# Second block's rows transposed before their norm, first weights split during the last expert, attention weights scaled as rows

## The chip, the cores and the metric

The kernel runs on one core of a Trainium2 chip. The metric is device microseconds from launch to end, the median of timed runs. Five engines work side by side and wait for one another by semaphores: TensorE (PE, matmuls; PEld is its weight load), VectorE (DVE), ScalarE (ACT), GpSimd (POOL) and SyncE (SP, which here issues the weight transfers).

## The reference, cut to what matters

Two transformer blocks on 256 rows of 1024, all in float32. Block 1 ends with a mixture of 32 experts and a norm; block 2 starts with a second norm, a projection, differential attention and a state space model, and ends with 32 larger experts.

```
x = x + hier_moe(rmsnorm(x, ffn_norm), ...)       # 32 experts, the last stage of block 1
x = rmsnorm(x, final_norm)                        # block 1's result, block 2's input
h = rmsnorm(x, norm1_g) * (1 + sc1) + sh1
q, k, v, u = split(h @ w_in)                      # 4 x 512 columns
p = softmax(causal(q k^T / 8))                    # per head two maps, 64 wide
att = p[0] - lam * p[1]                           # 4 heads
o = rmsnorm(att @ v, subln_g) * 0.8
mix = concat(o, s5(u)) @ w_out
x = x + g1 * mix
x = x + g2 * moe(rmsnorm(x, norm2_g)..., ...)     # 32 experts, top 4
out = rmsnorm(x, final_g)
```

## The kernel before

Rows stand on the partitions as `x_sb[128, 2, 1024]`, two blocks of 128 rows. Every weight passes through one pool of 20 slots of 1 MB (`Slots`, L230 to L292): SP issues a load as soon as a plan of all uses says that a slot will be free, so transfers run ahead of the work, and the first loads of the second expert stage are issued while block 2's mixer still runs. The order of the instructions on each engine is set by a planner that simulates them, except where `keep` holds the written order or `after(...)` puts what a block issues behind given instructions on the same engine. Each engine takes its own instructions in order.

The stages that the change touches, in order of time:

The last expert of block 1 (L1590 to L1646, e = 31): 4 weight tiles for gate and up, silu on ScalarE (L1614), `hid` on VectorE, a transposition, the copy `hdT` (L1631), 2 weight tiles for the down projection into `py`, and four copies of `py` into `ysb` on ScalarE (L1644). A conditional block for overfull experts (`spill1`, L1542, not taken) stands ahead of it. `heat` (L422) issues matmuls on the identity whose result nobody reads; it keeps TensorE working.

The join (L1647 to L1671): the scatter of the last four experts into `acc[0]` and `acc[1]` (two PSUM banks each, L1650), 14 heating matmuls, the split of the first weight tile u0, and the norms. A split (`split`, L446) makes of a float32 tile a high part, cast on ScalarE (L452), and a low part by subtraction on VectorE or GpSimd (L454), each in four pieces; a product then takes three matmuls (`mm3`, L461). Both norms of the join (block 1's last and block 2's first) are folded into one factor a row, from the sums of squares of `acc` and of `acc * fnorm`; the factor is put on a diagonal (L1670).

The turned rows (`turned`, L428; L1681): 16 products of x_sb, read with a stride of 8 elements, with that diagonal, which transpose and scale in one. Then, two k at a time, scale and shift by the modulation (L1687 to L1694), high part on ScalarE, low part on VectorE and GpSimd, and the splits of u1, q20 and k20 behind that.

The projections (`pair_T2`, L1708): 2 halves of 8 k of three matmuls each, half by half; u0 and u1 first, then the state space part and the q, k and v tiles in turn.

The attention heads: `d_scores` (L1813), `d_turn` (L1835), which puts the softmax denominators on diagonals and gets `p0/s0 - lam p1/s1` transposed by 6 products with them, `d_values` (L1852) and `d_out` (L1867), which scales and transposes the result by products with a diagonal of the row norm. Then the state space output, the gated unit, the output projection, the router and the 32 experts of block 2 (L2153 to L2236).

Of the kernel before, what the change touches and what calls it, by code (L numbers as in the profile page):

```python
# [19 lines left out]
D = 1024  # L20
# [289 lines left out]
def program(ctx: ExitStack, tc, T, out, plan):  # L310
# [1183 lines left out]
    sums = kpool.tile([128, 4, 2], F32, name="sums")  # L1494
    with tc.tile_pool(name="psm", bufs=1, space=PSUM) as pp, tc.tile_pool(name="m1s", bufs=2) as m1s, \
# [5 lines left out]
        px_ = lambda: pp.tile([128, 512], F32, name="px", tag="px")  # L1501
# [23 lines left out]
        def turn1(g):  # L1525
            pm = pp.tile([128, 2, 128], F32, name="pm")
# [63 lines left out]
        for e in range(32):  # L1590
            if e == 2:
                router2(px_())
            if e == 31:
                spill1()
            if e == 28:
                for _ in s5g:
                    pass
            g, e_ = divmod(e, 4)
            xe = xes[g][:, :, 32 * e_:32 * e_ + 32]
            pa = pp.tile([128, 2, 128], F32, name="pa")  # L1600
# [13 lines left out]
            act(sl, pa[:, 0], AF.Silu)  # L1614
# [13 lines left out]
            pm2 = pp.tile([128, 128], F32, name="pm2", tag="pm")  # L1628
# [26 lines left out]
        jk, jk2 = (W.alloc("jk").rearrange("p (a d) -> p a d", a=2) for _ in range(2))  # L1655
        af = [a.rearrange("p h c -> p (h c)") for a in acc]
        keep(tt(x_sb[:, 0], af[0], fnb, op=OP.mult))
        keep(act(jk[:, 0], af[0], AF.Square, accum_out=sums[:, 0, 0:1]))
        dgs = []
        for i in range(2):  # L1660
            c = slice(i, i + 1)
            keep(stt(jk2[:, i], x_sb[:, i], 1.0, x_sb[:, i], op0=OP.mult, op1=OP.mult, accum_out=sums[:, 1, c]))
            keep(ts(sums[:, 2, c], sums[:, 0, c], EPS / D, EPS * EPS, op0=OP.mult, op1=OP.add))
            keep(stt(sums[:, 3, c], sums[:, 1, c], 1.0 / D, sums[:, 2, c], op0=OP.mult, op1=OP.add))
            e_pool = keep(nc.gpsimd.tensor_tensor(sums[:, 3, c], sums[:, 3, c], mhalf[:, :1], op=OP.pow))
            if i == 0:
                keep(tt(x_sb[:, 1], af[1], fnb, op=OP.mult))
                e_act = keep(act(jk[:, 1], af[1], AF.Square, accum_out=sums[:, 0, 1:2]))
            dgs.append(jk2[:, i, :128])
            e_dve = keep(ts(dgs[i], ident, sums[:, 3, c], None, op0=OP.mult))  # L1670
# [614 lines left out]
```

## Time and profile before

| | us |
|---|---|
| timed runs, median (range) of 3 | 1894.46 (1894.25 to 1896.6) |
| the profiled execution, its own time | 1892.38 |
| its span, first to last instruction | 1890.6 |
| mean granted TensorE clock, share of full | 0.951 |
| TensorE busy, of the span | 1661.5 (88%) |
| VectorE busy | 680.5 (36%) |
| ScalarE busy | 351.8 (19%) |
| GpSimd busy | 171.3 (9%) |
| transfers, mean | 362 GB/s, 683.77 MB |

A row of a timeline has the start, the duration of what is merged in it, the engine, the line of the kernel, the operation, what it writes and reads, the shape and how many instructions; in brackets the idle time of the engine before it and what ended that. A float32 product on TensorE is two records (two passes), a transposition one. A row of a table of windows has the window, its length, and for each engine the busy time with the count of instructions, then the granted TensorE clock as a share of full speed, the share of the 16 DMA engines and GB/s. Busy TensorE is not TensorE at its peak, since the ends of matmuls are modelled.

### The profile page before, as it was taken

The numbers are of one execution on the slowest core, as the hardware profiler recorded it, in microseconds if no ns is written. First come the engines' busy times: TensorE is split into PE (matmuls) and PEld (weight loads), VectorE is DVE, ScalarE is ACT, GpSimd is POOL, SyncE is SP. The second block draws the span as 40 slices with busy tenths as digits, with TensorE's granted clock in tenths as the row PEclk, the third lists the DMA queues.
The fourth block names the chain that finished last, engine by engine and source line by source line (L and its number), as shares of the span: only waits on it lengthen the run. The fifth ranks groups of instructions, "written<-read, shape, count | busy, mean of one in ns | idle before, by whom it ended". The sixth has DMA issues, their size and how long they took to land. (4 is left out here: it accounts for less than half of the span.)

```text
span 1890.6 us, 27408 instructions
## 1 busy us (share of the span) xinstructions
PE 1661.5 (88%) x11497; PEld 906.0 (48%) x11497; DVE 680.5 (36%) x1411; ACT 351.8 (19%) x833; POOL 171.3 (9%) x150
## 2 busy tenths in 40 slices
PE   9988998978887776899799999999989989899887
PEld 8787867645553342598634333333323333333322
DVE  3886866553220000295622232222222222222221
ACT  3654533111111111254210000000000000000000
POOL 2863320000000000131200000000000000000000
PEclk9989999989998787799799999999999999999999
DMA  9445647999999999745599999999999999999994
GB/s 385 161 179 205 265 169 317 394 401 421 420 419 421 420 421 420 300 166 187 236 387 408 421 421 421 421 422 421 421 421 421 422 421 421 421 421 421 421 422 202
DMA packets 95219, 683.77 MB, mean 362 GB/s; under 512 B 10608, under 2 KB 10992, under 8 KB 12560
## 3 DMA queue, kind: packets, MB, share of 16 engines
q1 hardware_dynamic: 94464, 679.90, 87.7%
q8 instruction: 94, 1.54, 0.3%
q10 hardware_dynamic: 624, 2.03, 0.3%
q14 instruction: 37, 0.30, 0.0%
HBM read 680.84 MB, written 1.05 MB: 361 GB/s over the span
## 5 line engine op out<-in xcount | busy, mean ns | idle before, releaser
L2162 PE MATMUL pab<-wt,xe 128*64 128x512 f32 x2048 | 471.7, 598 | 18.4 <-DMA wt<-in_m2w_dram 18.4
L2162 PEld LDWEIGHTS pab<-wt,xe 128*64 128x64 f32 x2048 | 141.0, 137 | 300.8 <-issue 289.2
L2201 PE MATMUL py<-wt,hdT 128*64 128x512 f32 x1024 | 238.2, 598 | 19.8 <-DMA wt<-in_m2w_dram 17.1
L1606 PE MATMUL pa<-wt,xe 128*32 128x256 f32 x2048 | 151.0, 427 | 32.6 <-DMA wt<-in_m1w_dram 32.6
L2201 PEld LDWEIGHTS py<-wt,hdT 128*64 128x64 f32 x1024 | 69.5, 136 | 160.8 <-issue 108.7
L2175 DVE TENSOR_SCALAR gc<-pab 128x512 f32<-128x512 f32 x32 | 22.1, 691 | 339.5 <-PE pab L2168 339.5
L1606 PEld LDWEIGHTS pa<-wt,xe 128*32 128x32 f32 x2048 | 70.5, 120 | 102.8 <-DMA wt<-in_m1w_dram 43.1
L2207 DVE TENSOR_TENSOR b1b<-py,gate 64x512 f32<-64x512 f32 x64 | 44.1, 688 | 200.5 <-PE py L2201 188.6
L2177 ACT ACTIVATE sg<-gc 128x512 f32<-128x512 f32 x32 | 20.1, 630 | 461.2 <-DVE gc L2175 461.2
L1616 DVE TENSOR_TENSOR hid<-pa,sl 128x128 f32<-128x128 f32 x32 | 9.3, 290 | 240.8 <-ACT sl L1614 240.7
L1638 PE MATMUL py<-wt,hdT 128*32 128x256 f32 x1024 | 79.4, 446 | 15.0 <-issue 7.2
L402 POOL TENSOR_SCALAR r<-q 128x1 f32<-128x1 f32 x2 | 0.4, 191 | 946.6 <-DVE q L2253 946.6
L454 DVE TENSOR_TENSOR wh<-wt,wh 128x512 fp32r<-128x512 f32 (+2 forms) x57 | 76.5, 1372 | 10.8 <-ACT wh L452 10.6
L2048 PEld LDWEIGHTS pm<-gt,x_sb 128*128 128x128 f32 x512 | 62.4, 200 | 29.4 <-issue 29.0
L2048 PE MATMUL pm<-gt,x_sb 128*128 128x128 f32 x512 | 68.5, 290 | 5.1 <-DVE gt L2037 5.1
L2089 PE MATMUL pm<-b1b,st 128*128 128x512 f32 x120 | 63.7, 633 | 10.3 <-DVE b1b L2207 10.2
L1644 ACT COPY ysb<-py 32x256 f32<-32x256 f32 x128 | 46.4, 363 | 138.7 <-PE py L1638 137.5
L1522 PE MATMUL px<-gt,x_sb 128*128 128x128 f32 x256 | 65.5, 415 | 5.6 <-DVE s5t L1481 2.4
L2090 DVE TENSOR_TENSOR acc<-acc,pm 128x512 f32<-128x512 f32 x60 | 41.2, 687 | 77.7 <-PE pm L2089 77.7
L1522 PEld LDWEIGHTS px<-gt,x_sb 128*128 128x128 f32 x256 | 62.2, 335 | 12.2 <-issue 4.2
L452 ACT CAST wh<-wt 128x512 fp32r<-128x512 f32 (+2 forms) x65 | 62.0, 1019 | 14.6 <-issue 7.0
L464 PE MATMUL ps<-hTp,wh 128*128 128x256 f32 x480 | 63.4, 294 | 0.0
(577 smaller groups left out, 2007.8 us busy)
## 6 DMA issues: line engine op xcount, KB each, us to landing
wt<-in_m2w_dram SPq DMA_DIRECT2D x384, 1024.0 KB, 19.8
wt<-in_m1w_dram SPq DMA_DIRECT2D x192, 1024.0 KB, 17.7
wt<-in_wf_dram SPq DMA_DIRECT2D x44, 1024.0 KB, 8.0
wt<-in_wada_dram SPq DMA_DIRECT2D x24, 1024.0 KB, 5.0
x_sb<-in_x_dram SPq DMA_DIRECT2D x2, 512.0 KB, 4.2
out_dram<-y SPq DMA_DIRECT2D x4, 256.0 KB, 2.0
wt<-in_b_dram SPq DMA_DIRECT2D x3, 256.0 KB, 11.9
pars<-in_pars_dram ACTq DMA_DIRECT2D x1, 705.0 KB, 8.5
```

The costliest lines, as they stand in the source:

```text
L452: hi = nc.scalar.copy(h[:, a], w[:, a])
L454: lo = e.tensor_tensor(l[:, a], w[:, a], h[:, a].bitcast(F32), op=OP.subtract)
L464: mm(o, a[x], b[y], start=first and j == 0, stop=last and j == 2, skip_group_check=True)
L1522: mm(px[:, k], xkn[:, i, 4 * h + k], gts[g][:, i], start=(k == 0 and i == 0), stop=(i == 1), skip_group_check=True)
L1606: m_ = mm(pa[32 * q:32 * q + 32], xe[:, k], w[:, :, k % 2, 128 * q:128 * q + 128], start=(k == 0), stop=(k == 7), skip_group_check=True)
L1638: mm(py[32 * d:32 * d + 32], hdT[:, 32 * q:32 * q + 32], w[:, q % 2, 256 * d:256 * d + 256], start=(q == 0), stop=(q == 3), skip_group_che ...
L1644: m_copy = nc.scalar.copy(o, i)
L2048: mm(px[:, k], x_sb[:, i, 128 * kk:128 * kk + 128], gts[g][:, i], start=(k == 0 and i == 0), stop=(i == 1), skip_group_check=True)
L2089: mm(p, st2[g][:, i], ysb[g][:, 512 * d:512 * d + 512], start=True, stop=True)
L2162: last = mm(pab[a][64 * h:64 * h + 64], xe[:, k], w[:, 1024 * a + 512 * h:1024 * a + 512 * h + 512], start=(k == 0), stop=False, skip_grou ...
L2201: mm(py[d][64 * d:64 * d + 64], hdT[:, kk % 4, 64 * (kk // 4):64 * (kk // 4) + 64], w[:, kk % 2, 512 * d:512 * d + 512], start=(kk == 0), ...
L2207: tt(ysb[g][64 * e_:64 * e_ + 64, 512 * d:512 * d + 512], py[d][r_], gate2[r_], op=OP.mult)
```

## The change

Five edits. (1) u0 is split ahead of the last expert's matmuls, behind the copies of the expert before it on ScalarE and VectorE; u1 is split inside the last expert, behind its silu and hdT; all lower parts on VectorE. Two of the last expert's four copies to ysb go to VectorE. (2) Behind the scatter stand 3 heating matmuls for 14. The products with `fnorm` and the squares go half row by half row, each engine on another bank than the other. (3) The rows of x_sb are transposed unscaled, 16 transpositions (`rows`), while the sums for the norms still run; the factor is spread to a row on all partitions by two matmuls with the identity (`rb`), copied (`rbs`) and multiplied onto the turned rows (`times`) before the modulation (`high`, `low`); GpSimd has no part in it any more. The stage is written inside the expert stage's pools. (4) `pair_T2` goes k by k, both halves at each. (5) In `d_turn` the attention rows are scaled and combined as rows on VectorE and transposed by 3 transpositions; in `d_out` the same for the output, read from PSUM, so that the copy `osb` goes.

```diff
@@ last expert
             if e == 31:
                 spill1()
+                with after(m_copy, h_copy):
+                    prep2("u0")
...
-            act(sl, pa[:, 0], AF.Silu)
+            a_silu = act(sl, pa[:, 0], AF.Silu)
...
-            nc.vector.tensor_copy(hdT, pm2)
-            py = pp.tile([128, 256], F32, name="py")
+            h_copy = nc.vector.tensor_copy(hdT, pm2)
+            if e == 31:
+                with after(a_silu, h_copy):
+                    prep2("u1")
+            py = bank("py")[:, :256]
...
-                m_copy = nc.scalar.copy(o, i)
+                if e == 31 and d % 2:
+                    h_copy = nc.vector.tensor_copy(o, i)
+                else:
+                    m_copy = nc.scalar.copy(o, i)
@@ join
-        heat(px_, 14)
-        with after(m_copy):
-            prep2("u0", [nc.vector, nc.gpsimd, nc.vector, nc.gpsimd])
...
+        heat(px_, 3)
...
+        def rows(i):
+            for k in range(8):
+                keep(tr(pts[k // 2][:, k % 2, i * 128:(i + 1) * 128], xkn[:, i, k], ident))
+
+        def both_norms(i, whole):
+            q = sums[:, i]
+            c = lambda k: q[:, k:k + 1]
+            keep(tt(c(4), c(0), c(1), op=OP.add))
+            keep(ts(c(5), c(4), EPS / D, EPS * EPS, op0=OP.mult, op1=OP.add))
+            keep(stt(c(6), c(2), 1.0 / D, c(5), op0=OP.mult, op1=OP.add))
+            keep(nc.gpsimd.tensor_tensor(c(6), c(6), mhalf[:, :1], op=OP.pow))
+
+        sq = lambda i, h: keep(act(jh[:, h], acc[i][:, h], AF.Square, accum_out=sums[:, i, h:h + 1]))
+        tf = lambda i, h: keep(tt(x2[:, i, h], acc[i][:, h], f2[:, h], op=OP.mult))
+        tf(0, 0), sq(0, 1), tf(0, 1), sq(0, 0)
+        rows(0)
+        keep(act(js[:, 0], x_sb[:, 0], AF.Square, accum_out=sums[:, 0, 2:3]))
+        tf(1, 0), sq(1, 1), tf(1, 1), sq(1, 0)
+        rows(1)
+        both_norms(0, True)
+        keep(stt(js[:, 1], x_sb[:, 1], 1.0, x_sb[:, 1], op0=OP.mult, op1=OP.mult, accum_out=sums[:, 1, 2:3]))
+        both_norms(1, False)
+        rb = pp.tile([128, 2, 512], F32, name="rb", tag="acc0")
         for i in range(2):
...
+            keep(mm(rb[:, 0, 128 * i:128 * i + 128], sums[:, i, 6:7].to_broadcast([128, 128]), ident, start=(i == 0), stop=True,
+                    skip_group_check=True))
...
+        keep(nc.scalar.copy(rbs, rb[:, 0, :256]))
...
+        def times(j):
+            keep(tt(hv[:, j % 2], pts[j], rbs[:, None, :].to_broadcast([128, 2, 256]), op=OP.mult))
+
+        def high(j):
+            for a in range(2):
+                A, B = ab(2 * j + a)
+                keep(act(hp2[0][:, 2 * j + a], hv[:, j % 2, a], AF.Identity, scale=A, bias=B))
+
+        def low(j):
+            A, B = ab(2 * j + 1)
+            f = hv[:, 2 + j % 2]
+            e_ = keep(act(f[:, 1], hv[:, j % 2, 1], AF.Identity, scale=A, bias=B))
+            A, B = ab(2 * j)
+            keep(ts(f[:, 0], hv[:, j % 2, 0], A, B, op0=OP.mult, op1=OP.add))
+            return e_, keep(tt(hp2[1][:, 2 * j:2 * j + 2], f, hp2[0][:, 2 * j:2 * j + 2].bitcast(F32), op=OP.subtract))
+
+        times(0)
+        for j in range(4):
+            high(j)
+            if j < 3:
+                times(j + 1)
+            e_act, e_dve = low(j)
@@ behind the turned rows
-        with after(e_act, e_dve, e_pool):
-            prep2("u1", [nc.vector, nc.gpsimd] * 2)
+        with after(e_act, e_dve):
             prep2("q20")
@@ pair_T2
-            for b in range(2):
-                for k in range(8):
+            for k in range(8):
+                for b in range(2):
@@ d_turn
-            for m in range(2):
-                dg = fs.tile([128, 2, 128], F32, name="dg2", bufs=4)
-                for i in range(2):
-                    ts(dg[:, i], ident, st[:, 2, m, i:i + 1], None, op0=OP.mult)
...
+            for i, (a, e) in enumerate(((0, 128), (128, 384))):
+                ts(p0[:, a:e], p0[:, a:e], st[:, 2, 0, i:i + 1], None, op0=OP.mult)
+                stt(p0[:, a:e], p1[:, a:e], st[:, 2, 1, i:i + 1], p0[:, a:e], op0=OP.mult, op1=OP.add)
             pt = ps()
...
+            for a in (0, 128, 256):
+                tr(pt[:, a:a + 128], p0[:, a:a + 128], ident)
@@ d_values and d_out
-            nc.vector.tensor_copy(osb, po)
...
             for i in range(2):
-                ts(dg[:, i], ident, r[:, i:i + 1], None, op0=OP.mult)
+                ts(osb[:, i], po[:, i], r[:, i:i + 1], None, op0=OP.mult)
             pt = ps()[:, :S]
             for i in range(2):
-                mm(pt[:, 128 * i:128 * i + 128], osb[:, i], dg[:, i], start=(i == 0), stop=True, skip_group_check=True)
+                tr(pt[:, 128 * i:128 * i + 128], osb[:, i], ident)
```

## Rows read from the trace of the kernel before

**Rows 1.** Windows of 10 us where the second expert stage begins.
```profile
940.00:950.00 10.00, 10.00 (x50) 6.70 (x50) 1.37 (x4) 4.68 (x6) 0.00 (x0) 0.78 0.20 66
950.00:960.00 10.00, 10.00 (x50) 3.84 (x48) 0.00 (x0) 0.00 (x0) 0.00 (x0) 1.00 0.98 388
```

**Rows 2.** The last of the saturated windows of 30 us.
```profile
1830.00:1860.00 30.00, 28.01 (x119) 9.13 (x120) 7.67 (x12) 1.00 (x2) 0.00 (x0) 1.00 1.01 420
```

**Rows 3.** Windows by stage of block 2's mixer.
```profile
816.50:857.00 40.50, 38.42 (x317) 36.89 (x318) 35.82 (x67) 16.56 (x47) 4.24 (x3) 0.96 0.65 227
857.00:917.00 60.00, 58.07 (x711) 50.86 (x710) 32.98 (x69) 26.38 (x63) 7.60 (x12) 1.00 0.51 196
```

**Rows 4.** SyncE's issues of u0 and u1; median to landing, the same in both windows.
```profile
760.41 0.33 SPq L259 DMA_DIRECT2D wt<-in_wf_dram  x1
762.89 0.33 SPq L259 DMA_DIRECT2D wt<-in_wf_dram  x1
wt<-in_wf_dram SPq DMA_DIRECT2D x1, 1024.0 KB, 21.3
```

**Rows 5.** Timeline of ScalarE in the last expert.
```profile
780.86 0.28 ACT L1614 ACTIVATE sl<-pa 128x128 f32<-128x128 f32 x1 [14.22 <-PE pa L1606]
785.89 1.49 ACT L1644 COPY ysb<-py 32x256 f32<-32x256 f32 x4 [4.75 <-PE py L1638]
```

**Rows 6.** Timeline of the join, up to the projections u0 and u1.
```profile
786.75 3.63 PE L1650 MATMUL acc<-ysb,st 128*128 128x512 f32 x8
787.41 2.18 ACT L452 CAST wh<-wt 128x512 fp32r<-128x512 f32 x4
...
791.61 1.02 ACT L1658 ACTIVATE jk<-acc 128x1024 f32<-128x1024 f32 x1 [2.02 <-DVE x_sb L1657]
791.61 1.22 DVE L1662 SCALAR_TENSOR_TENSOR jk<-x_sb 128x1024 f32<-128x1024 f32 x1
792.53 0.19 ACT L1658 ACTIVATION_READ_ACCUMULATOR jk<-acc 128x1 f32 x1
...
792.76 0.15 DVE L1663 TENSOR_SCALAR sums<-sums 128x1 f32<-128x1 f32 x1
...
793.18 0.55 POOL L1665 TENSOR_TENSOR sums<-sums,mhalf 128x1 f32<-128x1 f32 x1 [1.61 <-DVE sums L1664]
...
795.44 7.92 PE L439 MATMUL ps<-jk,x_sb 128*128 128x128 f32 x32 [1.94 <-ACT jk L1668]
...
805.88 10.22 PE L464 MATMUL ps<-hT2p,wh 128*128 128x256 f32 x83 [0.57 <-DVE hT2p L1693]
```

**Rows 7.** TensorE's timeline; then groups by form (busy us, mean ns of one).
```profile
820.16 11.76 PE L464 MATMUL ps<-hT2p,wh 128*128 128x256 f32 x96
854.05 1.50 PE L1846 MATMUL ps<-dg,pr 128*128 128x128 f32 x12
916.46 1.03 PE L1950 MATMUL ps<-cst,x_sb 128*128 128x128 f32 x8
...
L1972 DVE TENSOR_TENSOR gm<-ps,gb 128x512 f32<-128x512 f32 x4 | 2.8, 688 | 7.0 <-PE ps L464 7.0
L1975 ACT ACTIVATE gm<-x_sb 128x512 f32<-128x512 f32 x4 | 2.5, 632 | 11.4 <-DVE x_sb L1974 11.4
L1807 DVE TENSOR_TENSOR th<-th,vz 128x256 f32<-128x256 f32 x4 | 1.7, 416 | 0.0
L469 ACT CAST cat<-th 128x256 fp32r<-128x256 f32 x4 | 1.6, 404 | 2.3 <-DVE th L1807 2.1
L1806 DVE TENSOR_SCALAR th<-th 128x256 f32<-128x256 f32 x4 | 1.1, 288 | 2.3 <-ACT th L1805 2.3
```

**Rows 8.** Granted clock in one window of 1 us during the turned rows.
```profile
798.00:799.00 1.00, 1.00 (x6) 1.00 (x5) 0.00 (x0) 0.00 (x0) 0.00 (x0) 0.50 0.00 0
```

**Rows 9.** TensorE's timeline at the first head's turn and the third head's scores.
```profile
845.39 0.77 PE L1846 MATMUL ps<-dg,pr 128*128 128x128 f32 x2 [1.78 <-ACT wh L452]
...
855.85 0.93 PE L1818 MATMUL ps<-qkT 64*128 64x128 f32 x8 [0.30 <-ACT qkT L390]
```

More of the change, by code (lines that the diff above doesn't have):

```diff
@@ L1500, in program @@
         slots4 = C("slot32").rearrange("p (a s) -> p a s", a=4)[:, None].to_broadcast([128, 2, 4, 32])
-        px_ = lambda: pp.tile([128, 512], F32, name="px", tag="px")
+        bank = lambda n: pp.tile([128, 512], F32, name=n, tag=n)
+        px_ = lambda: bank("px")
         s5g = s5_tables(s5p, px_)
@@ L1525, in turn1 @@
         def turn1(g):
-            pm = pp.tile([128, 2, 128], F32, name="pm")
+            pm = bank("pm")[:, :256].rearrange("p (i t) -> p i t", i=2)
             for i in range(2):
@@ L1599, in program @@
             xe = xes[g][:, :, 32 * e_:32 * e_ + 32]
-            pa = pp.tile([128, 2, 128], F32, name="pa")
+            pa = bank("pa")[:, :256].rearrange("p (a f) -> p a f", a=2)
             for k in range(8):
@@ L1650, in program @@
                 keep(mm(acc[i][:, h], st1[7][:, i], ysb[7][:, 512 * h:512 * h + 512], start=False, stop=True, skip_group_check=True))
-        heat(px_, 14)
-        with after(m_copy):
-            prep2("u0", [nc.vector, nc.gpsimd, nc.vector, nc.gpsimd])
[L1655 to L1658, printed above, removed]
@@ L1671, in program @@
-        W.drop()
+        heat(px_, 3)
+        jk, jk2 = (W.alloc("jk") for _ in range(2))
+        x2 = x_sb.rearrange("p i (h c) -> p i h c", h=2)
+        f2 = fnb.rearrange("p (h c) -> p h c", h=2)
+        js = jk.rearrange("p (a c) -> p a c", a=2)
+        jh = jk2.rearrange("p (a c) -> p a c", a=4)
+        pts = [bank(n).rearrange("p (a t) -> p a t", a=2) for n in ("pa", "pm", "py", "px")]
+        def rows(i):
+            for k in range(8):
+                keep(tr(pts[k // 2][:, k % 2, i * 128:(i + 1) * 128], xkn[:, i, k], ident))
@@ L1672, in program @@
+        W.drop(2)
     m1x.close()
@@ L1678, in ps @@
             return pp.tile([128, 512], F32, name="ps", tag="ps")
-        hp2 = both(halves("hT2p"), k8)
-        pts = turned(fs, ps, x_sb, None, dgs)
-        for k in range(0, 8, 2):
-            A, B = ([ab1[:, j, k + a:k + a + 1] for a in range(2)] for j in range(2))
-            hf = [jk2[:, k // 2 % 2, 256 * a:256 * a + 256] for a in (1, 2)]
-            for a in range(2):
-                keep(act(hp2[0][:, k + a], pts[k + a], AF.Identity, scale=A[a], bias=B[a]))
-            if k // 2 % 2 == 0:
-                keep(ts(hf[1], pts[k + 1], A[1], B[1], op0=OP.mult, op1=OP.add))
-            else:
-                e_act = keep(act(hf[1], pts[k + 1], AF.Identity, scale=A[1], bias=B[1]))
-            keep(ts(hf[0], pts[k], A[0], B[0], op0=OP.mult, op1=OP.add))
-            e_dve = keep(tt(hp2[1][:, k], hf[0], hp2[0][:, k].bitcast(F32), op=OP.subtract))
-            e_pool = keep(nc.gpsimd.tensor_tensor(hp2[1][:, k + 1], hf[1], hp2[0][:, k + 1].bitcast(F32), op=OP.subtract))
-        W.drop()
-        with after(e_act, e_dve, e_pool):
-            prep2("u1", [nc.vector, nc.gpsimd] * 2)
+        with after(e_act, e_dve):
             prep2("q20")
             prep2("k20", nc.gpsimd)
-            r = rstd(fs, sums[:, 0], D, 2, "r0")
+            r = rstd(fs, sums[:, :, 4], D, 2, "r0")
             for i in range(2):
@@ L1835, in d_turn @@
         def d_turn(h):
[L1836 to L1842 removed]
+            (p0, p1), st = hst[h]
+            for i, (a, e) in enumerate(((0, 128), (128, 384))):
+                ts(p0[:, a:e], p0[:, a:e], st[:, 2, 0, i:i + 1], None, op0=OP.mult)
+                stt(p0[:, a:e], p1[:, a:e], st[:, 2, 1, i:i + 1], p0[:, a:e], op0=OP.mult, op1=OP.add)
             pt = ps()
[L1844 to L1847 removed]
+            for a in (0, 128, 256):
+                tr(pt[:, a:a + 128], p0[:, a:a + 128], ident)
             ptb = fs.tile([128, 384], F32, name="ptb2")
```

33 lines of the change are left out of this document (9 added, 24 removed).

## Prediction

> **What bounds the kernel now.** I read the granted clock and the span first, then the ten-microsecond windows around the join of second mixer and second expert stage. [Rows 1] show transfers at 0.20 of the sixteen DMA engines in 940 to 950 and at 0.98 in the next window; [rows 2] is one of the thirty such windows between there and 1860, all at 1.00 to 1.02. So from about 950 the expert weights set the pace. The mixer does not: before 950 the weight slots are full and the queue waits for the first expert to empty one. Whatever brings that first expert forward brings the whole saturated stretch forward by as much. The window tables by stage then say what the mixer itself waits for: in 816.5 to 857 TensorE is busy 38.42 of 40.5 us and VectorE 35.82; in 857 to 917 TensorE 58.07 of 60 and VectorE 32.98 [rows 3]. TensorE work removed there counts nearly whole, VectorE work added before 857 does too. Between the last expert of block 1 and 806 neither holds: it is a chain of waits, read from the timeline.
>
> **The change, part by part.** Times are places in the profiled execution (1892.38 us, span 1890.6 plus 1.8 around it). The three timed runs have a median of 1894.46, so the sum is subtracted from that.
>
> *Last expert.* The first two weight tiles, u0 and u1, are issued at 760.41 and 762.89 and each lands 21.3 us later [rows 4]: 781.7 and 784.2. silu of the last expert runs at 780.86, the four copies to ysb from 785.89, 1.49 in all [rows 5]. In the forecast u0's four casts (2.18 us for four, [rows 6]) stand behind silu on ScalarE, run 781.7 to 783.9, and meet only idle time; their lower parts on VectorE (0.69 each) likewise. u1's casts run 784.2 to 786.4 and hold up the copies to ysb, of which ScalarE now has two (0.75) and VectorE two, behind u1's last lower part: ready at about 787.7 instead of 787.38, so the accumulating matmuls (3.63, [rows 6]) end near 790.9, 0.5 later than now. If the cover is missing (casts ahead of silu) it is rival B.
>
> *Norm and transposition.* Now: the diagonals wait for the row norms, 16 matmuls in two passes (32 records) take 7.92 us from 795.44, and the projections u0 and u1 end at 805.88 + 10.22 = 816.10 [rows 6]. The new chain: acc[0] is complete half-way through the accumulation, 789.1. One half product on VectorE must wait for the other engine's square on the same bank, as ScalarE's square waits 2.02 us for VectorE now [rows 6]; a square costs 0.63 [rows 7] and 0.19 for its sum [rows 6], a product 0.69 [rows 7], so row block 0 stands at 789.1 + 0.82 + 0.69 = 790.6 and its 8 transposes follow at the old strided pitch (7.92/32 = 0.25): 791.4 to 793.4. ScalarE goes on with the second square of block 0 (790.7), the square of the whole row (1.02 + 0.19, 791.9), one half square of block 1 (792.7); VectorE's last product ends 793.4 and the second 8 transposes 795.4. That is not what ends last: VectorE still has three small operations (0.15 each and their gaps, 0.5), the row square (1.22, with its sum 1.3), three more (0.5): 795.7; the power on GpSimd (0.55) 796.35, all [rows 6]; two broadcast matmuls in two passes (four records of 0.125, and an allowance of 0.3 until they are through) 797.1; the copy (0.40) 797.5; the first product with the broadcast row (0.69) 798.2; the first scaled row on ScalarE (0.40) 798.6. From there each pair of k needs on VectorE a product (0.69), a scale (0.29) and a subtraction of 512 (0.69, all [rows 7]): 1.67, and on ScalarE three of 0.40. Pair 0 is whole at 800.1, pair 3 at 805.1. The matmuls now go k first, so u0 follows: 12 x 0.1225 (11.76/96, [rows 7]) after the last pair, 806.6; u1 needs 48 x 0.1225 = 5.9 more and is already split: 812.5. Gain 3.6. Against it stands the clock: after 1.94 us without work at 795.44, the granted clock was 0.50, the lower level of 1.2 GHz, at 798 [rows 6, 8]. The new kernel has 3 heating matmuls where it had 14 and is sparse from 795.4 to 800. If u0's first pairs run at half clock they take 2.9 instead of 1.5 each, yet are paced by 1.67 anyway; bounds 0 and 3.8 (three pairs at half clock, ending 810.4), I take 1.0, nearer to the low end because now the low level lasts about 3 us. **Net 2.6.**
>
> *VectorE relieved.* Two of u1's lower parts and the end of the pair work 1.6 us sooner free VectorE before the projections. TensorE waits 1.78 us for the first head's diagonals at 845.39, behind a VectorE queue that is nearly always busy [rows 3, 9]. Bounds 0 and 1.78; less 0.4 for the longer chain ahead of the first transposition (a scale and a multiply-add instead of one diagonal) I take **1.2**.
>
> *Attention rows scaled.* A head's turn is 12 records in 1.50 now and becomes 3 transposes; eight contiguous transposes take 1.03 [rows 7], so 3 take 0.39. Saved 1.1 a head, 4.4 for four if nothing is late behind. After the second head something is: its score matmuls wait for the copy of the k projection [rows 9], so there 0.2; the last head stands among short matmuls with waits, 0.8; the others 1.0. **3.0**, bounds 0 and 4.4. On VectorE four diagonals go and two scales (at most 0.29) and two multiply-adds (at most 0.42, as the two-input operation of 256 in [rows 7]) come, at most +0.3 a head; the output step loses a copy of 256 from the accumulator bank, no shorter than a scale of 256. I set the two against each other, at nothing; what hides a rest is VectorE's idle 27 us of 60 after 857 [rows 3], and before it two heads would cost 0.6.
>
> The Trainium skill, TensorE: Matmul & The Clock Gate, Terms, says that trn2's transpose mode is four times faster for FP32. [Rows 7] show a transposition at 0.13 and a product at 2 x 0.125: half as long, by one pass instead of two. By the page a transposition would take a quarter of a product's 0.25, 0.06, and a turn save 0.2 us a head more: 1886.4. The rows decide, and are what the sum uses.
>
> *Output scaled as rows.* 4 records of 0.125 become 2 transposes of 0.13: 0.24 a head, 1.0 at most and 0 at least; with the waits on the norm there I take half, **0.5**. The accumulator bank is held longer, until the row scale instead of the copy; other banks hide it, at worst the time of one product, 0.69, a head.
>
> Sum 2.6 + 1.2 + 3.0 + 0.5 = 7.3: **1894.46 - 7.3 = 1887.2 us**, and 1885.1 on the profiled execution's own 1892.38.
>
> **Rivals.** *A is the forecast. B: ScalarE is parked.* The order on ScalarE is a planner's, and u0's casts are written ahead of the last expert. If they stand ahead of silu, silu waits for u0: 781.7 + 2.18 = 783.9 instead of 780.86, 3.1 with the lower parts on VectorE; hid, hdT, the down projection and the accumulation all wait behind. The 0.5 for u1 falls away: 7.3 + 0.5 - 3.1 = 4.7, so 1889.8. For it: the landing is later than silu by 0.8 us only. Against: the weights come in one stream, and u0 is behind every weight that silu needs; a planner that knows this puts silu first.
> The Trainium skill, PSUM — Partial Sum Buffer, Engine vs sequencer instructions, says that ScalarE, VectorE and GpSimd take their queue strictly in order. By that rule nothing overtakes a parked cast; no row here shows a cast parked on a weight.
>
> *C: every term whole.* 3.6 + 1.78 + 4.4 + 1.0 = 10.8: 1883.7. It needs the clock to hold and no wait behind any head.
>
> *D: the clock stays low through u0* (three pairs at half): 7.3 + 1.0 - 3.8 = 4.5, 1890.0.
>
> *E, slower: B, and the pause costs the clock.* With silu parked, TensorE has from 781 to 785 only its heating matmuls. If the clock falls there, the accumulation takes 7.3 instead of 3.6 and u0 has it too: 3.1 + 3.6 + 3.8 = 10.5 against gains of 3.6 + 0.5 + 1.2 + 3.0 + 0.5 = 8.8: +1.7, 1896.2. It decides once the clock is at 0.50 before 786. Against it: the pause is filled by 8 heating matmuls.
>
> *F: hidden by the transfers.* If the prefetch before 950 were what ends last, nothing would be gained, 1894.5. Against it: 0.20 busy in 940 to 950 [rows 1] means slots full and engines idle, for longer than the 7.3 us.
>
> **How the numbers follow.** A 0.44, C 0.14, B 0.20, D 0.05, E 0.10, F 0.07. What a measurement of this kernel can tell from no change is about 0.2%, 3.8 us. Below 1890.7 lie nearly all of A (0.42), C, two thirds of B (0.13) and of D (0.03): faster 0.72. E is within 3.8 us in half its cases and over it in the other: slower 0.05; same 0.23. The likeliest case alone runs from 1884 to 1890. The range goes from 1881.5, past C for costs taken too high, to 1893.5, past B and D; outside are E, F and tails, under 0.2.
>
> **What would show it.** ScalarE's casts of u0 behind silu and no idle gap before them that a weight ends (else B). The first u0 matmul near 799 and u1 ended near 812.5 to 813.5, counted from the same place in the last expert; the granted clock between 796 and 803. A turn of three records of 0.13. The gap before the first head's turn shrunk to some 0.5. The first matmul of the second expert stage, about 7 earlier, and the saturated stretch of the same length: if that stretch is longer, the reading of the bound is wrong. If the mixer is shorter and the end is not, F holds.

## The result: 1906.8 us, slower by 0.6%

The changed kernel takes 1906.8 us (median of ten runs, 1902.72 to 1911.23) against 1895.15 of the kernel before in the same session: ratio 1.006, 95% interval 1.0048 to 1.0072. Forecast was 1887.2. The profiled execution is 1910.64 us, span 1908.8. It reaches the last expert some 4 us later than the profile of before, in code that the change does not touch (the hid transposition of the expert ahead starts at 764.55, before at 760.56), so stretches are counted from that transposition; over all kernels measured here it starts anywhere from 759.89 to 766.64.

First the timeline of the changed kernel from the last expert to the projections (the counterpart of [rows 5, 6]): start, duration, engine, line, what it does; in brackets the idle time ahead of it and what ended that.

```profile
783.18 1.07 PE L1609 MATMUL pa<-wt,xe 128*32 128x256 f32 x16
...
792.88 2.18 ACT L452 CAST wh<-wt 128x512 fp32r<-128x512 f32 x4 [22.54 <-SPq L1545]
...
795.09 0.28 ACT L1617 ACTIVATE sl<-pa 128x128 f32<-128x128 f32 x1
...
796.29 0.47 PE L1632 MATMUL pm<-cst,hid 128*128 128x128 f32 x1 [12.04 <-DVE hid L1619]
...
804.37 3.70 PE L1659 MATMUL acc<-ysb,st 128*128 128x512 f32 x8
...
813.64 1.49 PE L1694 MATMUL rb<-cst,sums 128*128 128x128 f32 x4 [0.85 <-POOL sums L1680]
...
815.17 0.37 ACT L1697 COPY xe<-rb 128x256 f32<-128x256 f32 x1 [2.87 <-PE rb L1694]
...
816.30 1.09 ACT L1708 ACTIVATE hT2p<-jk,ab 128x256 fp32r<-128x256 f32 x2 [0.76 <-DVE jk L1703]
...
820.25 0.68 DVE L1703 TENSOR_TENSOR jk<-px,xe 128x512 f32<-128x512 f32 x1
...
821.08 14.07 PE L464 MATMUL ps<-hT2p,wh 128*128 128x256 f32 x96 [5.94 <-DVE jk L1703]
...
864.83 0.45 PE L1878 MATMUL ps<-cst,pr 128*128 128x128 f32 x1 [2.91 <-issue]
...
875.36 0.93 PE L1854 MATMUL ps<-qkT 64*128 64x128 f32 x8 [1.30 <-ACT qkT L390]
```

The gate and up products of the last expert are done at 784.25, but silu, which reads them, runs at 795.09, directly behind u0's four casts; TensorE stands 12.04 us. The casts themselves were released by SyncE at line 1545, the overflow branch that is not taken. Next, SyncE: issues of u0 and u1 among those of the last expert's tiles, their time to landing (windows around each issue), SyncE's events of that line between 740 and 800 (duration min/median/max, first and last start), and its waits there (total, times, longest).

```profile
749.50 0.33 SPq L259 DMA_DIRECT2D wt<-in_wf_dram  x1
751.98 7.77 SPq L259 DMA_DIRECT2D wt<-in_m1w_dram  x4
761.91 0.33 SPq L259 DMA_DIRECT2D wt<-in_wf_dram  x1
764.39 2.82 SPq L259 DMA_DIRECT2D wt<-in_m1w_dram  x2
```
```profile
wt<-in_wf_dram SPq DMA_DIRECT2D x1, 1024.0 KB, 19.8
...
wt<-in_wf_dram SPq DMA_DIRECT2D x1, 1024.0 KB, 20.7
```
```profile
L1545 SPq EVENT_SEMAPHORE  x8: 17/17/17, 782.7 to 792.7; - x8
```
```profile
SPq L1545 <- SPq L1545: 20.3, 5, 10.4
```

u0 landed at 749.50 + 19.8 = 769.3, 23.6 us ahead of its first cast. Loads follow the order of first use, so u0 now stands ahead of all six of the last expert's own tiles and u1 ahead of its two down tiles ([rows 4] had both behind all of them, 760.41 and 762.89). What the cast waits for is its destination. In the program u0's high half lies where the branch's body has its weight tile; that body loads it on all eight queues, and whoever writes the slot next waits for counts that include those loads. When the body is skipped, SyncE adds the counts itself, queue by queue, each only after what was issued on it before the branch has landed: the last load ahead of the branch is issued at 771.9 and lands 20.7 us later, the last count comes at 792.7, the cast at 792.88. The experiments test this.

Granted clock (third column from the end) at the normalised row and at u0's first matmuls: the lower level, 1.2 GHz, as in [rows 8]. Then TensorE's stretch from the last hid transposition to the scatter, first of the changed kernel, then of the kernel before: the stall let the clock fall there too, and 5.24 us became 8.08 at a mean of 0.62.

```profile
813.00:814.00 1.00, 0.35 (x1) 0.36 (x2) 0.58 (x5) 0.00 (x0) 0.86 (x2) 0.50 0.00 0
821.00:822.00 1.00, 0.93 (x4) 0.96 (x5) 1.00 (x5) 1.00 (x3) 0.84 (x2) 0.50 0.00 0
```
```profile
796.29:804.37 8.08, 8.08 (x58) 5.68 (x58) 3.11 (x6) 1.52 (x5) 0.00 (x0) 0.62 0.45 166
```
```profile
781.51:786.75 5.24, 5.24 (x57) 3.84 (x58) 0.29 (x1) 0.82 (x3) 0.00 (x0) 1.00 0.62 256
```

### The profile page after: what moved, and what is told of

Same layout as the page of the kernel before. It is cut to its first block, busy times and chain, and to the rows that moved or that the text cites. A ratio compares the mean times of both kernels' runs of the same rounds, so it can differ in the third digit from the quotient of the medians.

```text
span 1908.8 us, 27234 instructions
## 1 busy us (share of the span) xinstructions
PE 1658.4 (87%) x11419; PEld 901.5 (47%) x11419; DVE 682.5 (36%) x1415; ACT 354.5 (19%) x840; POOL 162.4 (9%) x142
## 5 line engine op out<-in xcount | busy, mean ns | idle before, releaser
L1609 PE MATMUL pa<-wt,xe 128*32 128x256 f32 x2048 | 147.1, 419 | 35.8 <-DMA wt<-in_m1w_dram 35.8
## 6 DMA issues: line engine op xcount, KB each, us to landing
wt<-in_m2w_dram SPq DMA_DIRECT2D x384, 1024.0 KB, 19.8
```

Of the source, the lines that this page charges most:

```text
L1609: m_ = mm(pa[32 * q:32 * q + 32], xe[:, k], w[:, :, k % 2, 128 * q:128 * q + 128], start=(k == 0), stop=(k == 7), skip_group_check=True)
```

## Experiments

Stretches read from TensorE's timeline of each profile, in us (A to D are stretches, not the prediction's rivals of those letters). A: from the hid transposition of the expert ahead to that of the last expert; B: from the same place to the scatter's end; C: scatter's end to the end of u1; D: from there to the first matmul behind the gated unit (the row of the gate, `grow`). Each stretch is of one execution. The kernel before, heads alone, turn alone and outputs alone have the same code in A to C; among them A and B differ by 1.1 us and C by 0.07. Granted clock differs in D from run to run, so D is good to some 2 us. Ratio to the kernel before, with its 95% interval, which reaches some 2 us to either side: what is smaller is read from the stretches or not at all.

| kernel | A | B | C | D | ratio |
|---|---|---|---|---|---|
| before | 20.95 | 29.82 | 25.72 | 76.83 | |
| after | 31.74 | 43.52 | 27.08 | 75.61 | 1.006 (1.0048, 1.0072) |
| own slots | 21.32 | 32.39 | 26.34 | 73.01 | 1.001 (0.9996, 1.0024) |
| splits put back | 21.44 | 30.39 | 28.32 | 75.74 | 0.9998 (0.9985, 1.0012) |
| heads alone | 20.05 | 28.91 | 25.79 | 75.32 | 0.999 (0.998, 1.0) |
| no branch | 16.70 | 29.37 | 26.90 | 75.56 | 1.0 (0.9987, 1.0013) |
| load order | 20.57 | 29.51 | 31.29 | 74.42 | 1.0018 (1.0007, 1.0029) |
| old pool's banks | 20.11 | 33.20 | 31.52 | 84.46 | 1.0101 (1.0087, 1.0116) |
| busy, same tile | 21.09 | 32.22 | 32.05 | 75.50 | 1.0051 (1.0037, 1.0066) |
| three together | 21.79 | 30.74 | 39.07 | 84.76 | 1.0122 (1.0107, 1.0137) |
| halves shared | 20.62 | 29.56 | 32.23 | 74.26 | 1.001 (0.9999, 1.0021) |
| busy, other bank | 21.99 | 32.51 | 25.23 | 74.58 | 1.0001 (0.999, 1.0011) |
| those two together | 20.91 | 29.86 | 29.62 | 74.56 | 1.0015 (1.0002, 1.0027) |
| old join, early u0 | 20.88 | 29.75 | 25.83 | 76.70 | 0.9998 (0.9986, 1.001) |
| u0 alone early | 21.81 | 30.76 | 24.88 | 75.92 | 0.9998 (0.9987, 1.0009) |
| turn alone | 20.78 | 29.65 | 25.75 | 77.05 | 1.0015 (1.0002, 1.0028) |
| casts behind silu | 21.29 | 31.17 | 26.97 | 75.56 | 1.0009 (0.9995, 1.0023) |
| behind silu, busy | 20.91 | 30.78 | 24.53 | 74.53 | 0.9997 (0.9983, 1.0011) |
| outputs alone | 21.17 | 30.04 | 25.78 | 79.51 | 0.9998 (0.9986, 1.0009) |
| join best, old turn | 21.11 | 30.98 | 24.98 | 77.92 | 1.0006 (0.9994, 1.0019) |

### What the casts wait for

```
+ first = [halves("wh") for _ in range(2)]   # ahead of spill1()
+ for p in first:
+     for t in p: keep(nc.gpsimd.memset(t[:, :1].bitcast(F32), 0.0))
  spill1()
  with after(m_copy, h_copy):
-     prep2("u0")
+     prep2("u0", into=first[0])             # u1 likewise
```

> The changed kernel, but the two halves that each of u0's and u1's splits writes take their slots ahead of the overflow branch (a one-column memset each on GpSimd), so that they lie apart from the three slots of the branch's body. Theory 1: u0's casts stand ahead of the last expert's silu on ScalarE and wait, not for u0's landing, but because their destination had been the body's weight slot: SyncE counts the skipped body's loads only after every transfer issued before the branch has landed. Then the 12.04 us in front of the last expert's hid transposition fall to under 1.5 us, and the time goes from 1.006 to 0.999 to 1.001 of the kernel before. Rival 1: the casts wait for u0 itself in the one stream of loads; the gap stays over 8 us and the ratio 1.004 to 1.007. Prediction's sum with the stall gone and every other term whole: 0.996.

Timeline with own slots: ScalarE's casts of u0, silu, then TensorE; and the granted clock over u0 and u1.

```profile
767.73 2.18 ACT L452 CAST wh<-wt 128x512 fp32r<-128x512 f32 x4
...
782.28 0.28 ACT L1621 ACTIVATE sl<-pa 128x128 f32<-128x128 f32 x1 [12.38 <-PE pa L1613]
...
782.94 0.33 PE L1636 MATMUL pm<-cst,hid 128*128 128x128 f32 x1 [0.72 <-DVE hid L1623]
...
785.86 1.07 PE L1648 MATMUL py<-wt,hdT 128*32 128x256 f32 x16 [1.70 <-DMA wt<-in_m1w_dram]
...
806.70 13.65 PE L464 MATMUL ps<-hT2p,wh 128*128 128x256 f32 x96 [5.94 <-DVE jk L1707]
```
```profile
806.00:808.00 2.00, 1.30 (x6) 1.33 (x7) 2.00 (x6) 1.87 (x4) 1.21 (x2) 0.50 0.01 4
808.00:811.00 3.00, 3.00 (x16) 3.00 (x16) 2.79 (x5) 3.00 (x6) 0.23 (x1) 0.50 0.00 0
811.00:813.00 2.00, 2.00 (x19) 2.00 (x19) 0.30 (x1) 2.00 (x4) 0.07 (x1) 1.00 0.00 0
```

Same casts, same place in the queue, same early load of u0, another address: they run at 767.73, directly behind the copies ahead of them, though SyncE adds the branch's counts only from 779.9 to 780.5 in this run; the gap of 12.04 is 0.72. The slot is the cause, as theory 1 said; a busy stream of loads is not. Two more runs bear it out, one with the splits written where they were and one without the branch (which leaves out the work for rows over an expert's capacity; this input has none).

```
- with after(m_copy, h_copy): prep2("u0")        # ahead of the last expert; u1 behind silu
+ with after(m_copy, h_copy):                    # behind the last expert's heat
+     prep2("u0", [nc.vector, nc.gpsimd, nc.vector, nc.gpsimd])
+ ... prep2("u1", [nc.vector, nc.gpsimd] * 2)    # behind the turned rows
```

> The changed kernel with u0's split put back behind the last expert and u1's behind the turned rows, each on VectorE and GpSimd as before; transposition, norm row and heads stay changed. Theory 1: no cast stands ahead of silu, the hid transposition comes as in the kernel before (idle under 1 us), ratio 0.998 to 1.001: the other edits bring little, since in the changed kernel's trace u0 and u1 end 27.1 us behind the scatter against 25.7 before. Prediction's terms whole: 0.997. Rival 1: the stall is not of the splits' place, ratio 1.004 or more.

```
- spill1()
```

> The changed kernel without the overflow branch of the first expert stage (leaves out the work for rows over an expert's capacity, which this input does not have). Theory 1: without the branch nothing counts skipped loads, so u0's casts run when u0 has landed (some 770 us) and the stall of 12 us is gone; so are the 4.7 us in which TensorE's sequencer stood at the branch: 1889 to 1892 us, ratio 0.997 to 0.9985. Rival 1: the casts wait for u0's landing in the stream, the stall stays above 8 us and only TensorE's 4.7 us go: ratio 1.003.

Neither has the stall (A 21.44 and 16.70). Without the branch A is 4.25 shorter than before, yet TensorE then stands 2.05 us in front of the down matmuls, at 786.11: their first tile was issued at 765.98 and took 20.0 us (the view names a low half on VectorE that ended then as well, which these matmuls don't read). B is only 0.45 shorter, which is within its spread. So TensorE's 5 us at the branch had for the most part been time in which tiles arrived. That run's expected 0.997 to 0.9985 was missed. Writing both splits behind silu, without slots claimed, is enough as well:

```
+ with after(a_silu, h_copy):     # behind the hid transposition
+     prep2("u0")                 # was: ahead of the expert
      prep2("u1")
```

> The changed kernel with both splits written between the last expert's hid transposition and its down matmuls, held behind silu only, and no slots claimed ahead; the halves of u0 then do not lie in the slot of the branch's weights. Theory 1: no stall in front of the hid transposition (under 1 us), 1.000 to 1.001, since the join is as with own slots. Rival: whatever is split ahead of the scatter waits for the branch's counts (792.7 us in the changed kernel), so the last rows' copies, which stand behind the casts, come 5 us or more later, and the ratio is 1.003 or more.

Its casts run from 782.16, right behind silu at 781.85, while the last of the branch's counts comes only at 789.4 there: their slot does not wait for them. With the stall gone by any of these ways 1.000 to 1.001 is left, not the forecast gain.

### Where the gain of the join went

> The changed kernel with own slots, and u0 and u1 accumulated in two banks of the first stage's own PSUM pool instead of the next pool's. Theory 4: u0's first matmul waits, not for its operands, but until the last tile of the old pool is read (the last product with the norm row), since the next pool opens when the old one is done: the idle time in front of it falls from 5.94 to about 3.3 us, and u1 ends 1 to 2.5 us sooner behind the scatter (26.4 us with own slots alone). Ratio 0.9995 to 1.0005. Rival: the products and the split rows come one pair at a time and pace the matmuls, so that what starts sooner ends no sooner: 26.4 us stays.

```
- p = ps()...                                   # a bank of the next pool
+ ub = pp.tile([128, 2, 512], F32, name="ub", tag="acc1")
+ p = ub[:, int(n[1])]...
```

```profile
802.87 0.58 PE L464 MATMUL ub<-hT2p,wh 128*128 128x256 f32 x1 [1.82 <-ACT hT2p L1712]
804.58 7.16 PE L464 MATMUL ub<-hT2p,wh 128*128 128x256 f32 x47 [1.13 <-DVE hT2p L1720]
...
816.63 7.98 PE L464 MATMUL ub<-hT2p,wh 128*128 128x256 f32 x48 [4.89 <-DVE s5d L1757]
```

Theory 4 is right about u0: from a bank of the old pool its first matmul starts 9.78 us behind the scatter instead of 12.69. The whole got slower by my own edit: u1 shares u0's tile and waits until u0 is copied out (4.89), and the next pool, with everything in it, opens only after u1 is copied too (D 84.46). The kernel before had the same wait, which the old join with u0 split early shows: its first diagonal is ready at 800.17 and its first matmul starts at 801.24, with the last square that reads the old pool (that matmul reads neither the square nor its buffer; the view names both jk).

```
+ first = halves("wh")                          # claimed ahead of spill1()
+ with after(a_silu, h_hid):                    # behind the last expert's matmuls
+     prep2("u0", [nc.vector, nc.gpsimd] * 2, into=first)
- with after(m_copy): prep2("u0", ...)          # in the old join; u1 stays there
```

> The kernel before with its own transposition and norm, the heads scaled as rows, and u0 alone split behind the last silu in slots of its own (u1 as before). What the change's first edit is worth without its stall, on the old join: VectorE is rid of 1.3 us and ScalarE of 2.2 us of u0 in front of the squares; if that is on the path, the first diagonal comes 1 to 2 us sooner behind the scatter (5.1 us there before) and the ratio is 0.998 to 0.9985 (heads alone 0.999). Rival: the squares and products of the norm set it whoever else is in the queues: 0.999 as with the heads alone.

```profile
799.89 0.28 DVE L1674 TENSOR_SCALAR jk<-cst,sums 128x128 f32<-128x128 f32 x1
...
800.99 0.19 ACT L1672 ACTIVATION_READ_ACCUMULATOR jk<-acc 128x1 f32 x1
801.24 7.91 PE L439 MATMUL ps<-jk,x_sb 128*128 128x128 f32 x32 [2.05 <-ACT jk L1672]
```

This run has the heads scaled as rows too. So on the old join the early split is worth nothing: C is 25.83 against 25.79 with the heads alone, and the expected 0.998 to 0.9985 was missed. Then the clock, twice:

> The changed kernel with own slots, and 18 idle 128x128 matmuls put between the two that make the norm row and u0's first, so that TensorE does not stand there. Theory 5: the 6 us pause lets the granted clock fall to 0.50 for some 5 us of u0, which is why u0 and u1 take 13.65 us against 11.76 for the same 96 matmuls at full clock; without the pause they take under 12.3 us and end 1.4 to 2 us sooner: ratio 1.000. Rival: the 13.65 us are waits for rows and weights, and stay.

> Own slots, and 18 idle matmuls between the norm row and u0's first matmul, this time into a tile of their own that nothing else reads (in the run before they shared the norm row's tile, whose copy then waited 5.4 us for them). Theory 5: without the pause the granted clock does not fall to 0.50, and u0 and u1 take under 12.3 us instead of 13.65 (11.76 for the same 96 at full clock): 1.4 to 1.9 us off own slots alone, ratio 1.000. Rival: the 13.65 us are waits for rows and weights, and stay, ratio 1.001.

```
+ hb = pp.tile([128, 2, 512], F32, name="hb", tag="acc1")   # first try: rb's second bank
+ for _ in range(18):
+     keep(mm(hb[:, 0, :128], ident, ident, start=True, stop=True, ...))
  rbs = ...
```

The first try told nothing of the clock: the copy of the norm row waited for the idle matmuls in its tile (idle 8.04 instead of 2.87), so the pause came behind them. In a tile of their own they do what the theory said for u0 and u1, which take 11.75 us, though the clock did fall, to 0.50 in 803 to 809, and was back at 1.00 when u0 began at 810.93; C falls by 1.1 of the 1.9, since the idle matmuls end 0.8 us later than u0 could have begun. The run with the casts behind silu and the same idle matmuls repeats it:

> The run before this one with 18 idle matmuls in a tile of their own between the norm row and u0's first matmul. Theory 5: u0 and u1 take 11.75 us instead of 13.65 at a clock that does not fall, so 1.9 us off its time: 0.999 to 1.000. Rival: casts and copies on ScalarE set the join, and it stays where it was.

```profile
791.72 3.70 PE L1658 MATMUL acc<-ysb,st 128*128 128x512 f32 x8 [0.78 <-DVE ysb L1650]
...
802.05 5.77 PE L1697 MATMUL hb<-cst 128*128 128x128 f32 x36
...
808.20 11.75 PE L464 MATMUL ps<-hT2p,wh 128*128 128x256 f32 x96 [0.39 <-DVE jk L1705]
```

Here the clock was at 0.50 in 802 to 805 and back from 806. 11.75 us for the same 96 instead of 13.65 to 14.36 in the runs with the pause, C 24.53: the most that any version got out of the new join is 1.2 us less than before. In this run the early splits take 1.0 of it back ahead of the join: the scatter waits 0.78 us for a copy to ysb, which stands on VectorE behind eight low halves.

Then the loads. With four slots claimed SyncE issues the last two down tiles only behind the branch, at 780.83, and TensorE waits 1.70 for one. Three runs put u0 and u1 behind the expert's tiles:

```
- with after(m_copy, h_copy): prep2("u0", into=first[0])    # and u1
+ with after(a_silu, h_hid):                                # behind the down matmuls
+     for n, t in zip(("u0", "u1"), first): prep2(n, into=t)
      # second run: prep2(n, [nc.vector, nc.gpsimd] * 2, into=t); third: and the idle matmuls
```

> The changed kernel with own slots for the two splits, and both splits written behind the last expert's down matmuls (held only behind its silu and its turned rows), so that u0 and u1 are loaded behind the last expert's tiles, as in the kernel before. Theory 3: with own slots alone the down matmuls stood 1.70 and 0.29 us for their tiles, which had gone behind u0 and u1; here both waits are under 0.2 us, the scatter ends 2 us sooner behind the expert ahead, ratio 0.9995 to 1.000 (own slots alone: 1.001). Rival: u0 and u1 then land too late, their casts stand ahead of the last rows' copies and squares on ScalarE, and the scatter or the norm comes later by 2 us or more: ratio 1.002.

> As the run with the load order of before (own slots, both splits behind the last expert's tiles), but every second low half goes to GpSimd, as in the kernel before. Theory 6: there the first turned rows waited 3.83 us for VectorE, which was still at the eight low halves (0.65 us each) of u0 and u1 when the scatter ended; with four of them gone (2.6 us) the wait is under 1.5 us, and the ratio falls from 1.0018 to 1.0005 or less. Rival: the wait was for u1's landing, which holds ScalarE's casts and with them the squares; it stays over 3 us, ratio 1.0015 or more.

> Both: shared low halves with the loads in the order of before, and the idle matmuls in a tile of their own. If theories 5 and 6 hold and add up, the stretch from the scatter's end to u1's is 24 to 25 us against 25.7 in the kernel before, ratio 0.998 to 0.9995. If the first turned rows still wait 3 us or more, 1.000 to 1.001.

B falls to 29.5, as theory 3 said, but C is 31.29: the rival was right that the norm comes later by 2 us or more, though not by the casts on ScalarE that it named. u0's and u1's low halves stand in front of the norm's first product on VectorE, which starts as they end. Theory 6 fell: sharing the halves with GpSimd made C no better (32.23). First the run with all eight on VectorE (groups of 786 to 796.5 us: busy, mean ns; then the first product), then the shared one:

```profile
L454 DVE TENSOR_TENSOR wh<-wt,wh 128x512 fp32r<-128x512 f32 x8 | 4.9, 684 | 0.3 <-ACT wh L452 0.3
...
793.55 0.69 DVE L1686 TENSOR_TENSOR x_sb<-acc,fnb 128x512 f32<-128x512 f32 x1
```
```profile
L454 POOL TENSOR_TENSOR wh<-wt,wh 128x512 fp32r<-128x512 f32 x4 | 6.3, 1611 | 30.2 <-ACT wh L452 30.2
L454 DVE TENSOR_TENSOR wh<-wt,wh 128x512 fp32r<-128x512 f32 x4 | 5.4, 1396 | 0.6 <-ACT wh L452 0.6
```

The third run, with TensorE kept busy as well, has 29.62 and 1.0015. Two runs tried to put other pieces together: load order, old pool and 8 idle matmuls; then u0 alone early (`first` with one pair, u1 back behind the turned rows) with 18.

> Own slots, the loads in the order of before, u0 and u1 in banks of the old pool, and 8 idle matmuls behind the norm row: the three steps that theories 3 to 5 name, with the change's other edits kept. If each is worth what its theory says and they add up, the span from the scatter's end to u1's is 22 to 23.5 us against 25.7 in the kernel before, and the time is 0.997 to 0.998 of it. If the first two and the clock overlap, 0.999. If the join is paced by ScalarE's casts and squares, no better than with own slots alone (1.001).

> The changed kernel with u0 alone split early, in two slots of its own, u1 split behind the turned rows with halves shared as in the kernel before, and 18 idle matmuls in a tile of their own behind the norm row. With four slots claimed, SyncE issued the last expert's two down tiles only behind the branch (780.8 us), and the scatter ended 32.4 us behind the hid transposition of the expert ahead, against 29.8 before. Theory 3b: with two slots it does not, so the scatter ends 29.8 to 30.8 us behind, and u1 25 to 26 us behind that: ratio 0.9985 to 0.9995. Rival: u1's casts and halves in the join cost what the early split of u1 gained; the join takes 27 us or more, ratio 1.000 to 1.001.

The first carries the flaws of its parts (low halves ahead of the norm, a tile shared by u0 and u1, idle matmuls in the norm row's tile, a late pool). The second has the stretches that theory 3b gave, or better (B 30.76, C 24.88), 55.64 us in all against 55.54 before, and not the ratio, 0.9985 to 0.9995: 0.9998. Its A is 0.86 longer, within the spread of A; the 0.84 us that C is shorter is less than the ratio can show.

### The heads

> The kernel before with the attention weights and the heads' outputs scaled as rows, nothing else. The prediction's terms for this (3.0 and 0.5 us): 1891.6 us, ratio 0.998. Theory 2, from the changed kernel's trace, where the heads lie only some 1.5 us nearer to the start of the join than before: ratio 0.999 to 1.0. Rival: the row scalings in VectorE's queue hold the next head's work, ratio above 1.0005.

> The kernel before with the attention weights alone scaled as rows (the outputs' scaling as before). Theory 2b: both heads' edits together gave 0.999; their trace shows TensorE waiting 2.05 us for the first scaled output, which stands in VectorE's queue behind the next head's rows. Without that edit the time is 0.998 to 0.999. The prediction's term for this edit alone (3.0 us): 0.9984. Rival: the row scalings hold the first turn (2.90 us idle against 1.78) and the next scores (1.30 against 0.30), and that is the loss: 0.9995 or more.

> The kernel before with the heads' outputs alone scaled as rows, attention weights by diagonals as before. Theory 2c: with attention rows alone the gain was nil, with both 1.5 us from u1's end to the gated unit, so the outputs' scaling carries it: 75.0 to 75.6 us there against 76.83 before, ratio 0.9985 to 0.9995. Rival: the two need each other (the shorter VectorE queue of both), and alone it gives nothing: 76.5 us or more, 0.9995 to 1.0005. The prediction's term for it alone was 0.5 us.

> The run with the casts behind silu and TensorE kept busy (0.9997), with the attention weights by diagonals as in the kernel before. By theory 2c nothing is lost in the heads, and the first turn comes about 1 us sooner: 0.999 to 0.9997. Rival: the two edits of the heads need each other, 1.000 to 1.001.

The edits are the change's own `d_turn` and `d_out`, both or one of them, on the kernel before; the last run is the one with casts behind silu and TensorE kept busy, with the `d_turn` of before. TensorE's windows over D, the kernel before and then the turn alone (length, then TensorE's busy time):

```profile
sum 76.83, PE 72.43 PEld 68.53 DVE 52.32 ACT 32.74 POOL 12.24; mean PE 36.21 PEld 34.27 DVE 26.16 ACT 16.37 POOL 6.12
```
```profile
sum 77.05, PE 67.94 PEld 63.93 DVE 53.44 ACT 32.80 POOL 11.93; mean PE 33.97 PEld 31.97 DVE 26.72 ACT 16.40 POOL 5.97
```

TensorE's work fell by 4.49 us, the stretch did not: all of it became waits. The timeline of the turn alone, at the first turn (VectorE, then TensorE), the third head's scores and the first output (VectorE, then TensorE):

```profile
849.77 0.55 DVE L1838 TENSOR_SCALAR pr<-pr,st 128x128 f32<-128x128 f32 x2
...
850.83 0.74 DVE L1839 SCALAR_TENSOR_TENSOR pr<-pr,st,pr 128x128 f32<-128x128 f32 x2
851.28 0.30 PE L1842 MATMUL ps<-cst,pr 128*128 128x128 f32 x1 [2.90 <-issue]
...
859.23 0.93 PE L1818 MATMUL ps<-qkT 64*128 64x128 f32 x8 [1.30 <-ACT qkT L390]
...
879.66 0.42 DVE L1859 COPY osb<-ps 128x256 f32<-128x256 f32 x1 [1.08 <-ACT jk L1857]
...
880.00 0.47 DVE L1866 TENSOR_SCALAR dgo<-cst,hr 128x128 f32<-128x128 f32 x2
...
880.43 0.77 PE L1869 MATMUL ps<-dgo,osb 128*128 128x128 f32 x2 [3.44 <-DVE dgo L1866]
```

The kernel before, at the first turn's diagonals and the first output:

```profile
845.00 0.87 DVE L1841 TENSOR_SCALAR dg<-cst,st 128x128 f32<-128x128 f32 x4
...
874.43 0.46 PE L1874 MATMUL ps<-dgo,osb 128*128 128x128 f32 x2 [0.19 <-DVE dgo L1871]
```

The first wait is 1.12 longer than in [rows 9]: TensorE now starts 1.51 us behind the start of the first scale (a scale, another instruction in VectorE's queue, a multiply-add), where it started 0.39 behind that of the first diagonal. The second is 1.00 longer, since the scores wait for the copy of the k projection whatever the turn costs. The third was 0.19: the first output's diagonal now stands on VectorE behind the next head's copy, an order that the planner chose. The expected theory, that the outputs' edit was the one that lost, fell: the turn alone gives nothing (1.0015, if anything slower), both together 0.999. Whether the outputs alone gain anything is open: 0.9998, but in its profile the granted clock dipped to a mean of 0.74 in 889 to 902, which makes its D of no use. The last combination is no better (1.0006). It has the new join with the old turn, and its first turn waits as long as in the kernel before:

```profile
846.98 0.46 PE L1884 MATMUL ps<-dg,pr 128*128 128x128 f32 x2 [1.78 <-ACT wh L452]
```

So that wait goes with the turn, not with the join. No version tried is faster than the kernel before by more than a measurement can tell; the heads alone come nearest.

## Why the prediction was wrong

**Parking of ScalarE** was the prediction's rival B, with the right place and queue and a wrong price. The step that failed is that "u0's four casts (...) stand behind silu on ScalarE": they stood ahead of it. That rival took u0's landing for what releases them (3.1 us, 1889.8); a slot of the branch's body did, and the last hid transposition came 10.8 us later (stretch A, 31.74 against 20.95). The argument against it, "u0 is behind every weight that silu needs", was wrong too: loads go in the order of first use, and the edit moved the first use. SyncE's waits at the branch (19.2 us) could be read in the kernel before; the prediction did not ask who could be queued for its counts. What rival E foresaw came on top, in another place: with silu parked the clock fell, and the down products and idle matmuls behind the stall took 2.84 us longer (8.08 against 5.24), while the accumulation that it had priced at 7.3 ran at full clock (3.70). Together these make the 13.7 us by which stretch B grew; the medians of the whole kernel are 11.65 us apart.

The Trainium skill, PSUM — Partial Sum Buffer, Engine vs sequencer instructions, has ScalarE's queue strictly in order; here the trace agrees, silu at 795.09 right behind a cast that waited 22.54 us.

**Norm and transposition, net 2.6, and VectorE relieved, 1.2.** The chain was sized well: the first scaled row was forecast 7.7 us behind the scatter (798.6 less 790.9) and came at 8.2 (816.30 less 808.07). What failed is "The matmuls now go k first, so u0 follows", pair by pair: u0 did not start with pair 0 but after the last pair's product, at 13.0, since its bank belongs to the next pool; and the clock, at 0.50 from 813 on, stayed there through that wait and into u0: 14.07 us for 96 matmuls instead of 11.76. Stretch C was forecast at 22.6 (812.5 less 790.9, and 1.0 for the clock) against 25.72 before; it took 27.08, and 24.53 at best with the clock back before u0. The 0.5 put down for what u1's splits delay ahead of the norm was 1.0 in the run behind silu, busy (B less A 9.87, before 8.87). The wait of 1.94 in [rows 6] was the same rule, read as a wait for the norm. The gap ahead of the first turn, forecast to shrink to 0.5, grew to 2.91. The relief was worth nothing (1.78 with the new join and the old turn, as before), and the longer chain ahead of the first transposition, put at 0.4, cost 1.12.

**Attention rows, 3.0, and output, 0.5.** The busy time saved was sized right (4.4 at most, 4.49 measured), what is late behind it was not. The wait behind the second head was foreseen: 0.2 of its 1.1 us was to be left, and nothing was. Underpriced was the first turn's longer chain, and not foreseen an output that stands behind another head's copy; there 1.0 a head had been set down. The turn alone, forecast at 0.9984, measured 1.0015 (1.0002 to 1.0028); with the outputs it is 0.999 (0.998 to 1.0), and stretch D 1.5 us shorter, inside its spread, instead of 3.5.

**The bound** held: from the first matmul of the second expert stage to the end it is 945.68 before and 947.20 after; what comes later there ends later by as much, within 1.5 us. Rival F did not occur.

## To carry to other kernels

An instruction moved ahead in an in-order queue brings along everything that it may wait for, its destination's earlier owners among them; a slot that an untaken branch could have written is released late, so ask of each early write whose slot it gets. Moving a first use moves its load, past the loads of the step that it was meant to hide behind. Work removed from the busiest engine counts only if what replaces it elsewhere is ready sooner; and an early operand is worth nothing while its PSUM pool is not open.

## Not expected of the hardware

Skipping a branch cost SyncE 20.3 us in five waits, the longest 10.4. Low halves on VectorE took 684 ns each alone and 1396 while GpSimd ran the same operation (1611): four and four took longer than eight on VectorE. The Trainium skill, GPSIMD Engine Reference, Specifications, says that GpSimd's SBUF interface is shared with VectorE and contended for when VectorE has two inputs there, which agrees. With own slots the pause of 5.94 us ahead of u0 left TensorE at 0.50 until about 811, well into u0; 18 idle matmuls in it took 1.9 to 2.2 us off u0 and u1, and 1.1 and 2.4 off C.
